# Two gate tiles computed from the input before its norm, and the decays' chain moved into the first pairs, in a one-core hybrid layer

## The chip, the cores and the metric

The kernel runs on one core of a Trainium2 chip. The metric is the device time of one execution in microseconds (us). TensorE (PE in the profile's rows; PEld is its weight load) multiplies matrices into PSUM, VectorE (DVE) and ScalarE (ACT) do elementwise work, GpSimd (POOL) does almost nothing here, and SyncE (SP) issues the loads and stores.

## The reference, cut to what matters

One layer over 2048 positions of 1024 features, in float32:

```python
h = rmsnorm(x, norm_mix_w)                     # x * rsqrt(mean(x*x) + eps) * norm_mix_w
proj = h @ w_in
u_b, u_c, u_h, z, xbc, dt_raw = split(proj)
y_a = u_b * causal_conv3(u_c * u_h)
xs, bm, cm = split(silu(causal_conv4(xbc) + bias))
dt = softplus(dt_raw + dt_bias)                # 16 heads; decays come from cumsum(dt * a) in chunks
y = ssd_scan(xs, dt, a, bm, cm) + d * xs
y_b = grouped_rmsnorm(y * silu(z)) * ssd_norm_w
x = x + concat(y_a, y_b) @ w_out
out = rmsnorm(x + square(relu(rmsnorm(x) @ w_up)) @ w_down)
```

The norm's root is one number per position. A column of `x * norm_mix_w` times a matrix, multiplied by that number afterwards, is the same as the product of the normalised column.

## The kernel before

**Precision.** Each float32 operand is split into a rounded part (`hi`: `uh` for activations, `whi` for weights, a copy on ACT) and a remainder (`lo`: `ul`, `wlo`, a subtraction on DVE). `mm3` (L113 to L115) makes one product out of three matmuls: `whi*uh`, `whi*ul`, `wlo*uh`. `split_w` is at L100 (ACT) and L101 (DVE), the split of activations at L204 and L205.

**Halves, blocks, pairs.** The sequence is two halves of 1024 positions, each two blocks of 512 (`bb` 0 and 1). Features lie on partitions, 8 slices of 128 (`k`), and a weight tile is 1024 x 128. The input projection works on *pairs* of weight tiles by a scheme of seven products instead of eight over two blocks and two tiles (`chain`, L269 to L271: seven products of four slices, 84 matmuls of 512 columns). The pairs are named by kind: `z` (gate, SiLU), `x` (the scan's convolution: six passes on DVE, L651), `ch` (short convolution's input), `b` (its multiplier). `first_half` runs them in the order of `PAIRS`; while one pair runs, the weights of the next are split, and after each of the seven products a hook lets a generator take one step: `late` is the preparation of the second half's blocks (squares L347, sums L349 and L352, root and reciprocal L170 and L171, scaling L368, differences L208). In the last pair the hook also refills the activation tiles for the second half (L319, L320).

**The start.** `start` loads block 0 and the weights of the first four `z` tiles (24 to 27), which are not done as pairs but as plain products (`group`), because the first pair's sums over both blocks do not exist yet. `begin_block` is a generator: squares (L448 for block 0, L453 for block 1), sums of squares (`acc`, L455 and L458), sum over partitions on PE (`reduce`, tile `pst`, L131), root, reciprocal and two diagonal tiles (`root`, L143 to L151), spread over all partitions by two matmuls (`spread`, tile `prb`, L177, copied to `facc` at L180), then for each slice the scaling by root and `norm_mix_w` in place (L467) and the split. `group(0)` multiplies three tiles, then the fourth; `dt_part` follows for block 0: 16 small-output matmuls into `pd` (L591) with the split weight `wdt` (L571, L572), a copy `dts<-pd` (L595), transposes (`pt`), some 25 small instructions on DVE for softplus, cumulative sums by a matmul (`pc`), exponentials, and stores. Meanwhile block 1 goes through `begin_block`; then `begin_sums` builds the sums over the blocks while `group(1)` runs, and `dt_part` for block 1 goes on into the first pair.

**Order.** The lines of code are issued in the order in which the generators are stepped; a scheduler then fixes an order for each engine's queue when the kernel is built, and each engine works its queue off in that order. Tiles come from rings of buffers, and a tile's new owner waits for the last reader of the old one: three raw weight tiles (`wraw`), four split ones, four `utmp` tiles for squares, diagonals and z, two `tp` banks of PSUM for the small products.

Of the kernel before, what the change touches and what calls it, by code (L numbers as in the profile page):

```python
# [11 lines left out]
F32 = mybir.dt.float32  # L12
# [11 lines left out]
KD = D // P  # L24
# [15 lines left out]
def trunk(ctx: ExitStack, tc: tile.TileContext, x, w_in, w_dt, w_out, w_up, w_down, cvec, hrow, out):  # L40
# [352 lines left out]
    class Proj(Seven):  # L393
# [1 line left out]

        stored = hm_d

        PAIRS = "ch0 ch1 b0 x0 x8 ch2 ch3 b2 x2 ch4 ch5 b4 x4 x10 ch6 ch7 b6 x6 z4 z6".split()
        LATER = "z0 x0 z4 ch0 ch1 b0 x8 ch2 ch3 b2 x2 ch4 ch5 b4 x4 x10 ch6 ch7 b6 x6 z6 z2".split()
        FIRST = {"z": 24, "x": 32, "b": 0}  # L400

# [35 lines left out]
            return self.e(name).rearrange("p (a t) -> p a t", a=2)  # L437


        def begin_block(self, bb):  # L440

            xt = self.xt[bb]
            st = Rstd(self.up, self.tmp, D, TB)
            acc = self.facc()
            for m, t in enumerate(xt):
                if bb == 0:
                    sq = self.wide("sq")
                    nc.scalar.activation(sq, t, AF.Square)  # L448
                    sq = [sq[:, 0], sq[:, 1]]
                else:  # L450
                    sq = [acc if m + i == 0 else self.tmp("sq") for i in range(2)]
                    for i in range(2):
                        nc.scalar.activation(sq[i], t[:, i], AF.Square)  # L453
                if m == 0:
                    nc.vector.tensor_tensor(out=acc, in0=sq[0], in1=sq[1], op=ALU.add)  # L455
                else:
                    for i in range(2):
                        nc.vector.tensor_tensor(out=acc, in0=acc, in1=sq[i], op=ALU.add)  # L458
                yield
            st.reduce(acc)  # L460
            st.root()
            yield
            r = st.spread(acc)
            yield
            for k in range(KD):
                t = xt[k // 2][:, k % 2]
                nc.vector.scalar_tensor_tensor(  # L467
                    out=t, in0=t, scalar=col(C_NMIX, k), in1=r, op0=ALU.mult, op1=ALU.mult
                )
                self.fill(("b11", "b21", "b12", "b22")[2 * bb + k // 4], k % 4, t)  # L470
                yield
# [25 lines left out]
                if k % 2:  # L497
                    yield

        def group(self, bb, ws, tiles, work, tag="mm"):  # L500

            pm = [psum(tag, "pm", accs[tag]) for _ in tiles]
            for k in range(KD):
                for p, i in zip(pm, tiles):
                    mm3(p, ws[i][0][:, k, :], ws[i][1][:, k, :], *self.block(bb, k), k, KD)
                next(work, None)
            for p, i in zip(pm, tiles):
                o = self.tmp("z")
                nc.scalar.activation(o, p, AF.Silu)
                nc.sync.dma_start(sz_d[0][:, i, bb * TB : (bb + 1) * TB], o)  # L510

        def start(self):

            self.xt = [[self.raw("x0") for _ in range(KD // 2)], []]
            for k, t in zip(range(0, KD, 2), self.xt[0]):
                nc.sync.dma_start(t, x[0, :, k : k + 2])
            ahead = self.plain(w_in, (24, 25, 26))
            next(ahead)
            work = self.begin_block(0)
            for m in range(KD // 2):  # L520
                next(work)
            for m in range(KD // 2):
                t = self.wide("x1")
                nc.sync.dma_start(t, x[1, :, 2 * m : 2 * m + 2])
                self.xt[1].append(t)
            next(work)
            ws = []
            for _ in range(3):
                ws += take(ahead, 1)
                next(work)  # L530
            self.dt_weights()
            for _ in work:
                pass
            work = self.begin_block(1)
            last = self.plain(w_in, (27,))
            next(last)
            for bb in range(NBB):
                dts = self.dt_part(bb)
                self.group(bb, ws, (0, 1, 2), work)
                if bb == 0:  # L540
                    ws += take(last)
                    self.group(bb, ws, (3,), work, "mw")
                    self.bias()
                    for _ in dts:
                        next(work, None)
                    for _ in work:
                        pass
                    work = self.begin_sums()
                else:
                    ahead = self.weights(0, self.PAIRS[0])  # L550
                    next(ahead)
                    next(dts)
                    got = take(ahead, 3)
                    self.group(bb, ws, (3,), work, "mw")
                    got += take(ahead)
                    for _ in dts:
                        next(work, None)
                    for _ in work:
                        pass
            return got  # L560

        def dt_weights(self):
# [214 lines left out]
        def first_half(self, ws):  # L777
            self.last_sums()
            late = self.prepare(1, x, C_NMIX)
            for m, what in enumerate(self.PAIRS):  # L780
# [8 lines left out]

                def after(name):  # L790
                    next(late, None)
                    if last:
                        self.refresh(name)

# [811 lines left out]
```

## Time and profile before

| | us |
|---|---|
| median of 3 runs | 2670.18 (2669.47 to 2673.78) |
| the profiled execution | 2667.12 |
| its span in the trace | 2665.4 |
| PE busy | 2603.0 (98%) |
| DVE busy | 1911.8 (72%) |
| ACT busy | 1432.6 (54%) |
| PE's first matmul of a tile | at 19.68 |
| PE's first matmul of a pair | at 76.64 |

All times of the trace count from the span's start. A row of a timeline gives start, duration, engine, line, operation and operands, and in brackets how long the engine had been idle and what ended that. Matmuls overlap in the trace: what one costs in a run of them is the distance of their starts, not the duration shown.

### The profile page before, as it was taken

To read this page: it belongs to the slowest core of one execution; us is meant where nothing else is said; L and a number is where in the kernel's file an instruction comes from. 1 tells how busy PE (TensorE), PEld (TensorE's weight loads), DVE (VectorE), ACT (ScalarE), POOL (GpSimd) and SP (SyncE) were. 2 spreads that over 40 slices of the span, in tenths; PEclk is the share of its full clock that TensorE was granted. 3 is DMA by queue.
4 is the path that set the end of the run, shared out by engine and by line. 5 is a ranking of instruction groups with operands and counts; after the bars stand their busy time and mean duration, and the time that the engine had idled before them with its cause. 6 is when DMAs were issued, how large, how long until landed. Compare 5 with 4: busy or idle time off the path is not lost. (4 is left out here: it accounts for less than half of the span.)

```text
span 2665.4 us, 33577 instructions
## 1 busy us (share of the span) xinstructions
PE 2603.0 (98%) x12026; PEld 2125.4 (80%) x12026; DVE 1911.8 (72%) x2586; ACT 1432.6 (54%) x2176; POOL 145.0 (5%) x162
## 2 busy tenths in 40 slices
PE   7999999999999999998998999999999999999998
PEld 5778888778887888787887888788887888888887
DVE  7997677667667666666659755765558877888985
ACT  6644345766567566757316555755555444444443
POOL 0000000011111001111000000000000000000001
PEclk9999999999999999999999999999999999999999
DMA  3585335655555589876597944644448554665762
GB/s 145 188 307 188 136 142 187 191 164 170 173 161 171 165 265 266 251 213 210 187 323 260 331 154 162 223 173 160 143 165 283 159 158 146 208 215 169 246 206 70
DMA packets 288262, 522.27 MB, mean 196 GB/s; under 512 B 25696, under 2 KB 141408, under 8 KB 288096
## 3 DMA queue, kind: packets, MB, share of 16 engines
q1 hardware_dynamic: 288096, 520.14, 58.6%
q8 instruction: 94, 1.54, 0.2%
q14 instruction: 72, 0.59, 0.1%
HBM read 349.65 MB, written 170.39 MB: 195 GB/s over the span
## 5 line engine op out<-in xcount | busy, mean ns | idle before, releaser
L269 PE MATMUL px<-uh,whi 128*128 128x512 f32 x1672 | 657.4, 393 | 10.4 <-ACT pw L277 5.4
L271 PE MATMUL px<-uh,wlo 128*128 128x512 f32 x1672 | 651.8, 390 | 2.1 <-DVE wlo L101 2.1
L270 PE MATMUL px<-ul,whi 128*128 128x512 f32 x1672 | 651.9, 390 | 0.0
L101 DVE TENSOR_TENSOR wlo<-wraw,whi 128x1024 fp32r<-128x1024 f32 x230 | 234.5, 1020 | 209.2 <-ACT whi L100 203.6
L269 PEld LDWEIGHTS px<-uh,whi 128*128 128x128 f32 x1672 | 314.4, 188 | 86.0 <-ACT pw L277 8.0
L100 ACT CAST whi<-wraw 128x1024 fp32r<-128x1024 f32 x230 | 204.0, 887 | 316.3 <-PE px L270 189.2
L271 PEld LDWEIGHTS px<-uh,wlo 128*128 128x128 f32 x1672 | 314.3, 188 | 69.2 <-DVE wlo L101 2.9
L270 PEld LDWEIGHTS px<-ul,whi 128*128 128x128 f32 x1672 | 314.4, 188 | 63.8
L269 PE MATMUL py<-uh,whi 128*128 128x512 f32 x836 | 326.9, 391 | 1.9 <-DVE acc L973 1.6
L270 PE MATMUL py<-ul,whi 128*128 128x512 f32 x836 | 325.6, 389 | 0.0
L100 ACT CAST whi<-s 128x1024 fp32r<-128x1024 f32 x210 | 219.7, 1047 | 197.0 <-PE py L270 69.6
L271 PE MATMUL py<-uh,wlo 128*128 128x512 f32 x836 | 325.4, 389 | 0.0
L101 DVE TENSOR_TENSOR wlo<-s,whi 128x1024 fp32r<-128x1024 f32 x210 | 255.6, 1217 | 84.8 <-ACT whi L100 81.5
L113 PE MATMUL pm<-uh,whi 128*128 128x512 f32 (+1 forms) x648 | 253.1, 392 | 2.1 <-ACT uh L204 2.1
L114 PE MATMUL pm<-ul,whi 128*128 128x512 f32 (+1 forms) x648 | 250.3, 386 | 0.0
L115 PE MATMUL pm<-uh,wlo 128*128 128x512 f32 (+1 forms) x648 | 249.9, 386 | 0.0
L269 PEld LDWEIGHTS py<-uh,whi 128*128 128x128 f32 x836 | 156.9, 188 | 35.8 <-DVE acc L973 2.0
L271 PEld LDWEIGHTS py<-uh,wlo 128*128 128x128 f32 x836 | 156.9, 188 | 33.0 <-DVE wlo L101 0.3
L270 PEld LDWEIGHTS py<-ul,whi 128*128 128x128 f32 x836 | 157.0, 188 | 32.2
L269 PE MATMUL pw<-uh,whi 128*128 128x512 f32 x418 | 163.5, 391 | 0.7 <-ACT pw L277 0.7
L270 PE MATMUL pw<-ul,whi 128*128 128x512 f32 x418 | 162.7, 389 | 0.0
L271 PE MATMUL pw<-uh,wlo 128*128 128x512 f32 x418 | 162.7, 389 | 0.0
(221 smaller groups left out, 3744.7 us busy)
## 6 DMA issues: line engine op xcount, KB each, us to landing
hid_d<-e SPq DMA_DIRECT2D x96, 512.0 KB, 4.7
rh<-hid_d SPq DMA_DIRECT2D x96, 512.0 KB, 4.4
wraw<-w_in SPq DMA_DIRECT2D x68, 512.0 KB, 4.0
wraw<-w_up SPq DMA_DIRECT2D x64, 512.0 KB, 4.4
wraw<-w_down SPq DMA_DIRECT2D x104, 256.0 KB, 3.7
dec<-rd_d SPq DMA_DIRECT2D x32, 512.0 KB, 5.4
wraw<-w_out SPq DMA_DIRECT2D x32, 512.0 KB, 5.0
x_d<-xt SPq DMA_DIRECT2D x64, 256.0 KB, 3.3
```

Of the source, the lines that this page charges most:

```text
L100: nc.scalar.copy(hi, raw)
L101: eng.tensor_tensor(out=lo, in0=raw, in1=hi.bitcast(F32), op=ALU.subtract)
L113: nc.tensor.matmul(out, whi, hi, start=(k == 0), stop=False)
L114: nc.tensor.matmul(out, whi, lo, start=False, stop=False)
L115: nc.tensor.matmul(out, wlo, hi, start=False, stop=(k == nk - 1))
L269: nc.tensor.matmul(p, hi, h[0], start=bool(first and k == 0), stop=False, **kw)
L270: nc.tensor.matmul(p, hi, h[1], start=False, stop=False, **kw)
L271: nc.tensor.matmul(p, lo, h[0], start=False, stop=(k == len(g) - 1), **kw)
```

## The change

`unscaled` makes the split of `x * norm_mix_w` for the eight slices of block 0, without the norm's root: `hi` by a multiply on ACT, `lo` in one DVE instruction that multiplies and subtracts. It puts them where block 1's slices will lie later. The first two `z` tiles are multiplied from these (`group` with `block`), and each of the two results is multiplied by the spread root (`self.r`) on DVE as it leaves PSUM, ahead of the SiLU. Tile 24's weights are loaded directly after the first quarter of block 0; tiles 26 and 27 are multiplied from the normalised block. The weights of the decays (`dt_weights`) are made after that; of `dt_part` only the first step (the 16 matmuls and the copy `dts<-pd`) is issued in `start`, and the rest goes step by step into the hooks of the first pairs. In `PAIRS`, `z4` and `x0` come first and `x6` is now the last but one.

```diff
-        PAIRS = "ch0 ch1 b0 x0 x8 ch2 ch3 b2 x2 ch4 ch5 b4 x4 x10 ch6 ch7 b6 x6 z4 z6".split()
+        PAIRS = "z4 x0 ch0 ch1 b0 x8 ch2 ch3 b2 x2 ch4 ch5 b4 x4 x10 ch6 ch7 b6 x6 z6".split()
...
+        def unscaled(self, k, t):
+
+            i, j = WHERE["b12" if k < 4 else "b22"]
+            p = self.places[k % 4]
+            p[i] = self.place(i)
+            hi, lo = (a[:, j] for a in p[i])
+            nc.scalar.mul(hi, t, col(C_NMIX, k))
+            nc.vector.scalar_tensor_tensor(
+                out=lo, in0=t, scalar=col(C_NMIX, k), in1=hi.bitcast(F32), op0=ALU.mult, op1=ALU.subtract
+            )
+            return hi, lo
...
         def begin_block(self, bb):
...
+            if bb == 0:
+                self.first = [self.unscaled(k, xt[k // 2][:, k % 2]) for k in range(KD)]
+                yield
             st.reduce(acc)
             st.root()
             yield
-            r = st.spread(acc)
+            r = self.r = st.spread(acc)
             yield
...
-        def group(self, bb, ws, tiles, work, tag="mm"):
+        def group(self, bb, ws, tiles, work, tag="mm", block=None):
...
-                    mm3(p, ws[i][0][:, k, :], ws[i][1][:, k, :], *self.block(bb, k), k, KD)
+                    hi, lo = block[k] if block else self.block(bb, k)
+                    mm3(p, ws[i][0][:, k, :], ws[i][1][:, k, :], hi, lo, k, KD)
                 next(work, None)
             for p, i in zip(pm, tiles):
                 o = self.tmp("z")
+                if block:
+                    nc.vector.tensor_tensor(out=o, in0=p, in1=self.r, op=ALU.mult)
+                    p = o
                 nc.scalar.activation(o, p, AF.Silu)
...
         def start(self):
...
-            for k, t in zip(range(0, KD, 2), self.xt[0]):
-                nc.sync.dma_start(t, x[0, :, k : k + 2])
-            ahead = self.plain(w_in, (24, 25, 26))
-            next(ahead)
+            load = lambda m: nc.sync.dma_start(self.xt[0][m], x[0, :, 2 * m : 2 * m + 2])
+            load(0)
+            ahead = [self.plain(w_in, (24,)), self.plain(w_in, (25, 26))]
+            next(ahead[0])
+            for m in range(1, KD // 2):
+                load(m)
+            next(ahead[1])
+            ahead = itertools.chain(*ahead)
             work = self.begin_block(0)
...
+            ws = take(ahead, 1)
             next(work)
-            ws = []
-            for _ in range(3):
-                ws += take(ahead, 1)
-                next(work)
-            self.dt_weights()
+            ws += take(ahead, 1)
+            next(work)
+            next(work)
+            last = self.plain(w_in, (27,))
+            next(last)
+            self.group(0, ws, (0, 1), work, block=self.first)
+            ws += take(ahead)
+            ws += take(last)
             for _ in work:
                 pass
+            self.dt_weights()
+            self.bias()
+            dts = [self.dt_part(bb) for bb in range(NBB)]
+            next(dts[0])
             work = self.begin_block(1)
-            last = self.plain(w_in, (27,))
-            next(last)
-            for bb in range(NBB):
-                dts = self.dt_part(bb)
-                self.group(bb, ws, (0, 1, 2), work)
-                if bb == 0:
-                    ws += take(last)
-                    self.group(bb, ws, (3,), work, "mw")
-                    self.bias()
-                    for _ in dts:
-                        next(work, None)
-                    for _ in work:
-                        pass
-                    work = self.begin_sums()
-                else:
-                    ahead = self.weights(0, self.PAIRS[0])
-                    next(ahead)
-                    next(dts)
-                    got = take(ahead, 3)
-                    self.group(bb, ws, (3,), work, "mw")
-                    got += take(ahead)
-                    for _ in dts:
-                        next(work, None)
-                    for _ in work:
-                        pass
+            self.group(0, ws, (2,), work)
+            self.group(0, ws, (3,), work, "mw")
+            for _ in work:
+                pass
+            work = self.begin_sums()
+            self.group(1, ws, (0, 1, 2), work)
+            ahead = self.weights(0, self.PAIRS[0])
+            next(ahead)
+            next(dts[1])
+            got = take(ahead, 3)
+            self.group(1, ws, (3,), work, "mw")
+            got += take(ahead)
+            for _ in work:
+                pass
+            self.dts = itertools.chain(*dts)
             return got
...
                 def after(name):
                     next(late, None)
+                    next(self.dts, None)
```

## The prediction

> **What bounds the kernel now.** I read the page first, then the timelines of ScalarE (ACT), VectorE (DVE) and TensorE (PE) over the first 110 us, where the change lies, then the waits and the busy time by stretch of the pairs that follow.
>
> ```profile
> span 2665.4 us, 33577 instructions
> PE 2603.0 (98%) x12026; PEld 2125.4 (80%) x12026; DVE 1911.8 (72%) x2586; ACT 1432.6 (54%) x2176; POOL 145.0 (5%) x162
> ```
>
> PE is the bound: what is to be won are the spots where it stands still or runs slowly. The largest in the edited code is the start. In the timelines' rows (start, duration, engine, line, operation, count, idle time before and what ended it) ACT comes first, then DVE, then PE.
>
> ```profile
> 5.88 1.06 ACT L448 ACTIVATE sq<-x 128x1024 f32<-128x1024 f32 x1 [3.59 <-DMA x<-x]
> 10.91 1.05 ACT L100 CAST whi<-wraw 128x1024 fp32r<-128x1024 f32 x1 [0.21 <-DMA wraw<-w_in]
> 11.98 1.28 ACT L143 ACT_TABLE_LOAD   x1
> 17.61 0.59 ACT L180 COPY facc<-prb 128x512 f32<-128x512 f32 x1 [0.82 <-PE prb L177]
> 19.01 0.62 ACT L204 CAST uh<-x 128x512 fp32r<-128x512 f32 x1 [0.29 <-DVE x L467]
> ```
>
> ```profile
> 6.97 0.69 DVE L455 TENSOR_TENSOR facc<-sq 128x512 f32<-128x512 f32 x1 [5.83 <-ACT sq L448]
> 8.21 4.46 DVE L458 TENSOR_TENSOR facc<-facc,sq 128x512 f32<-128x512 f32 x6 [0.55 <-ACT sq L448]
> 15.43 1.29 DVE L151 TENSOR_TENSOR diag<-ident,rs 128x512 fp32r<-128x512 f32 x2
> 18.89 1.22 DVE L101 TENSOR_TENSOR wlo<-wraw,whi 128x1024 fp32r<-128x1024 f32 x1
> 24.76 2.73 DVE L467 SCALAR_TENSOR_TENSOR x<-x,cv,facc 128x512 f32<-128x512 f32 x4
> 27.41 2.49 DVE L205 TENSOR_TENSOR ul<-x,uh 128x512 fp32r<-128x512 f32 x4
> ```
>
> ```profile
> 12.73 1.87 PE L131 MATMUL pst<-ones_r,facc 128*128 128x1 f32 x8 [12.73 <-DVE facc L458]
> 16.17 1.40 PE L177 MATMUL prb<-diag,ones_r 128*128 128x512 f32 x2 [1.57 <-DVE diag L151]
> 19.68 1.65 PE L113 MATMUL pm<-uh,whi 128*128 128x512 f32 x3 [2.12 <-ACT uh L204]
> 24.97 0.63 PE L114 MATMUL pm<-ul,whi 128*128 128x512 f32 x1
> 25.39 0.55 PE L115 MATMUL pm<-uh,wlo 128*128 128x512 f32 x1
> 26.25 0.40 PE L114 MATMUL pm<-ul,whi 128*128 128x512 f32 x1
> 26.48 0.40 PE L115 MATMUL pm<-uh,wlo 128*128 128x512 f32 x1
> ```
>
> PE gets its first product at 19.68 us, after squares, sum, root, spread and scaling. Until about 25.7 two starts lie 0.42 us apart (24.97 to 25.39), later 0.23 (26.25 to 26.48): half the rate. Then it runs almost without a hole to the first pair, while the next norm (block 1) hides behind group 0:
>
> ```profile
> 39.01 0.92 PE L131 MATMUL pst<-ones_r,facc 128*128 128x1 f32 x7
> ...
> 76.64 0.50 PE L269 MATMUL px<-uh,whi 128*128 128x512 f32 x1
> ```
>
> ```profile
> 43.98 0.59 ACT L180 COPY facc<-prb 128x512 f32<-128x512 f32 x1 [1.84 <-PE prb L177]
> 45.44 0.63 ACT L204 CAST uh<-x 128x512 fp32r<-128x512 f32 x1
> 49.78 0.58 ACT L595 COPY dts<-pd 32x512 f32<-32x512 f32 x1 [2.13 <-issue]
> ```
>
> **The change, step by step.** I walk the queues in the order of the built changed kernel, with the durations above. In a run of equal instructions the next starts 0.67 us after the last for scaling on DVE (2.73 for four), 0.60 for a difference, sum or diag, 1.14 for a wlo (1.22 less the overlap); on ACT 0.53 (512 wide) and 0.95 (1024).
>
> *Start.* The five loads of 512 KB came between 5.88 and 10.91, 1.26 us apart; weight 24 now comes second, at 7.1. ACT: square to 6.9, two uh to 8.0, whi to 9.0. DVE must now do eight ul beside the eight sums: per slice k a ul and a sum, 1.27 us. The first ul ends at 8.3, the second at 9.0, wlo at 10.2, then ul2 to ul7 at 11.5, 12.75, 14.0, 15.25, 16.5, 17.8; the sum of squares is whole at 17.1 (before: 12.7). PE starts at 9.0, 10.7 us earlier, but three products per k at the half rate take 1.28 us, no faster than DVE delivers; at 18.0, 22 products and pst have gone through, which at full rate are 22 x 0.23 + 0.8 = 5.8 us of work. So 3.2 of the 9.0 us are lost.
>
> *Norm of block 0.* Root at 18.3 (its table load stands behind the two whi at 17.0), wlo of 25 and 26 between, diag to 21.7, copy to 22.9: 4.7 us later than the copy that ended at 18.2. PE covers this with the rest of tiles 0 and 1, 26 products plus prb, done at 24.6. That cover is not quite long enough: ul of the scaled block comes at 26.3, and DVE then owes 8 scalings (5.3), 8 ul (4.8), two multiplies out of PSUM (1.2, by the 0.6 of a sum), wlo of 27 (1.14) and about 1.1 of small ones: 13.5 us, to 36.4. PE waits for ul (1.2 at 25, 1.5 near 30, 1.6 near 34) and wlo (0.6): 5.0 us together. Group 0 and the 16 pd of the decays are through at 44.2; the two multiplies are in that 13.5. On SP the load of w_dt now stands behind those of tile 27 and of the first pair's weights and waits for a diag buffer; by the 1.26 us a load it lands near 24 and is wanted at 35, so it costs nothing unless it is 11 us late. POOL has no part in it.
>
> *Norm of block 1: the new wait.* On ACT the copy dts<-pd stands ahead of seven of the eight squares of block 1. pd needs wdt, at the end of that DVE queue, so it runs from 36.7 to 40.3, the squares from 40.9 to 44.7 and the sums to 45.9. PE has by then run out of work: behind the last product of tile 3 stand pst, prb and only then block 1. From 45.9: pst 0.8, root and small ones 0.8, diag 1.3, prb 0.5, copy 0.6 (after a 1.28 us table load and a z, which fit beside it), scaling 0.75, uh 0.62: first product at 51.4. So 44.2 to 51.4 is empty but for 1.2 us: 6.0 us lost. Before, this chain took 39.01 to 46.1 and hid behind tile 3 and pd.
>
> *The clock after it.*
>
> ```profile
> 1216.97:1220.38 3.41, 1.26 (x7) 1.13 (x8) 3.30 (x5) 3.39 (x5) 0.49 (x1) 1.00 0.75 216
> 1220.40:1223.80 3.40, 3.40 (x9) 2.64 (x8) 2.99 (x3) 2.50 (x5) 2.29 (x2) 0.50 0.96 246
> ```
>
> In these rows (stretch, then busy us of PE, PEld, DVE, ACT, POOL, granted clock) PE was busy 1.26 of 3.41 us, and in the next 3.4 us it had half the clock. The new wait holds 1.2 us of work in 7.2 us, so half the clock for 3.4 to 6 us after it, about 2.0 us lost; 0 if it stays up, 3 if it takes longest. The Trainium skill ("TensorE: Matmul & The Clock Gate", Part 1, The two states you'll see) gives half rate only after at least one idle window of about 3.4 us, and by that rule, with pst and prb inside, the 2.0 would be 0. The trace disagrees: a stretch that was 37% busy was enough. The same section's free-running window agrees with the steps of 3.4 us here.
>
> *Sum to the first pair.* Before: 76.64. Less 19.7 at the start, about 2.7 at half rate (13 products at 0.20) and 0.7 in small gaps, that is 53.5 us of PE work (with the second pst and prb). The changed kernel does the same, 1.0 less for pc, pr and one pt that go among the pairs, 1.2 more for the first pst and prb, which now lie inside: 53.7. Then 9.0 + 53.7 + 3.2 + 5.0 + 6.0 + 2.0 = 78.9, and the 1.0 comes later: **3.3 us behind**. Bounds: 1.3 (no half clock) to 5.3 (the clock comes up only behind the first pst, which puts the first norm 2 us later).
>
> *The first pairs.* A pair is 84 products x 0.227 = 19.1 us. DVE is the near-bound there:
>
> ```profile
> L101 DVE TENSOR_TENSOR wlo<-s,whi 128x1024 fp32r<-128x1024 f32 x14 | 17.1, 1223 | 0.6 <-ACT whi L100 0.4
> L651 DVE SCALAR_TENSOR_TENSOR cacc<-buf,cv,cacc 128x1024 f32<-128x1024 f32 x12 | 15.4, 1282 | 0.0
> L368 DVE SCALAR_TENSOR_TENSOR nb<-nb,cv,facc 128x512 f32<-128x512 f32 x16 | 11.3, 746 | 0.2 <-DMA nb<-x 0.2
> L208 DVE TENSOR_TENSOR nb<-nb 128x512 f32<-128x512 f32 x16 | 10.5, 686 | 0.0
> L171 DVE RECIPROCAL facc<-facc 128x512 f32<-128x512 f32 x2 | 6.7, 3347 | 0.0
> ```
>
> ```profile
> 96.29 0.22 DVE L619 SCALAR_TENSOR_TENSOR dts<-dts 128x64 f32<-128x64 f32 x1
> 96.42 0.69 DVE L696 TENSOR_TENSOR cc<-py,s 128x512 f32<-128x512 f32 x1
> ```
>
> ```profile
> 134.00:154.00 20.00, 20.00 (x90) 16.57 (x89) 13.84 (x21) 4.77 (x7) 0.57 (x1) 1.00 0.74 277
> 154.00:173.00 19.00, 17.95 (x78) 14.18 (x77) 19.00 (x25) 11.03 (x14) 2.34 (x3) 1.00 0.77 273
> 173.00:193.00 20.00, 17.89 (x78) 14.17 (x77) 19.80 (x27) 10.42 (x13) 2.24 (x3) 1.00 0.93 354
> ```
>
> ```profile
> PE px L271 <- DVE wlo L101: 2.1, 2, 1.5
> ```
>
> The views are the groups by line, a piece of DVE's timeline, the busy time by stretch and the waits. From 154 to 193 DVE is full and PE lacks 1.05 + 2.11 us, mostly waiting for wlo; a stall also hides some 0.16 us of the last product's modelled end, so about 4.5 us in all can come back. Why there: x0 and x8 (six L651 each, 7.7 us) meet there with the second half's preparation (L368, L208). In the new order z4, which has neither, comes first and x8 sixth, and the decays' two chains (some 25 small instructions at 0.13, 96.29 to 96.42, about 3.5 us each) move in. Every pair costs DVE 7.6 us (three wlo and a half one 4.0, four half sums 2.4, two adds 1.2); x0 in second place adds 7.7, a chain 3.5, a reciprocal 3.3, seven sums and a lo of the preparation 4.8: 27 us against 19.1. But DVE enters the pairs 3.5 us nearer to PE than before, and walking its queue I find every wlo of pairs 2 to 4 in time, by little; the one for b0's second product stands behind eight nb steps of the pair before and comes at about 161 where 159 is wanted. The chains' own pc has 0.4 us to spare on PE; what DVE is later than that, PE waits. Their ten small stores now lie among the loads of lx on SP; nothing reads them in this half. So I take 2 us of stalls for the 4.5: **2.5 us back**; bounds 4.5 back and 2 worse.
>
> *End of the first half.* x6 now stands last but one, so up to 7.7 us of L651 fall into the pair in which DVE refills the next block:
>
> ```profile
> 460.00:480.00 20.00, 18.07 (x78) 14.11 (x77) 15.96 (x19) 15.39 (x22) 0.00 (x0) 1.00 0.84 284
> ```
>
> ```profile
> PE px L269 <- ACT s L693: 1.4, 1, 1.4
> ```
>
> DVE has 4.0 of 20 us free, so it may end 3.7 late. PE waits only through ACT's queue (the 1.4 us): **1.2 us lost**, bounds 0 and 3.7.
>
> **Sum:** 3.3 - 2.5 + 1.2 = 2.0 us slower. The profiled execution took 2667.12 (span 2665.4 and 1.7 around it); it lies 3.06 under the median of 2670.18, which becomes about **2672.2**. A difference under 0.2% (5.3 us) cannot be told from none by a measurement of this kernel, whose three runs spread over 4.3 us.
>
> **Rivals.**
> 1. *The start's gain stays* (faster). If block 1's squares reach ACT before pd, or pst fits ahead of tile 3's end, the 6.0 and the 2.0 are gone: 2664.2. For it: the scheduler's order was meant to hide this. Against: pst stands behind tile 3's last product, and the squares behind dts<-pd. Chance 0.07.
> 2. *DVE becomes the bound in pair 2* (slower). With x0 and both chains, DVE's 27 us exceed the pair by 7.9; it takes 3.5 from its lead, and the rest, 4.4, is PE's as soon as wlo for pair 3 is later than its first product. Nothing comes back, so 2.0 + 2.5 + 4.4 = 8.9: 2679. For it: the full DVE rows above. Against: x's sums can trail behind wlo. Chance 0.15.
> 3. *Both ends of the half and the slow clock cost more* (first norm 2 us later, refill 3.7 late): 2.0 + 2.0 + 2.5 = 6.5: 2676.7. Chance 0.10.
> 4. *No half clock after the new wait*: 2.0 back: 2670.2. For it: the wait is not quite empty, 1.2 us of work lie in it; against it the 1216.97 row. The Trainium skill's rule named above speaks for it. Chance 0.13.
> 5. *Weight 24 lands no earlier than its 10.91* although issued second, and the early products do little: start 2 us later, 2674. Against: loads land in order here. Chance 0.05.
>
> **How the numbers follow.** My forecast has the remaining 0.50, at 2672.2, with its own range 2669 to 2675. The range over all, 2667.5 to 2678.5, takes in rivals 3 to 5, and the bound of 4.5 back; it leaves out rival 1 and the upper part of rival 2. Faster by over 0.2% is rival 1: 0.07. Slower by over 0.2% is rivals 2 and 3, less what falls short, 0.23 in all. The rest, 0.70, is within 0.2%.
>
> **What would show it.** First product near 9 us; facc<-prb near 23; the second pst near 46 with PE empty for some 6 us around it and half the clock behind; the first px near 79; PE's lack in the first seven pairs about half of before's. I am wrong if the second pst comes before tile 3 ends, or if DVE's wlo holds PE in pairs 2 and 3 for more than 2 us.

## The result, and the profile after

| | before | after |
|---|---|---|
| median, 9 runs each | 2670.22 us (2664.28 to 2676.84) | 2682.49 us (2676.19 to 2692.42) |
| the profiled execution | 2667.12 | 2682.08 |

The ratio is 1.0043, 95% interval 1.0031 to 1.0055: slower by some 12 us, where the forecast was 2 and the range ended at 2678.5. The direction was right, the size was not.

The page of the changed kernel, its span and its line of busy time:

```profile
span 2680.1 us, 33586 instructions
PE 2608.6 (97%) x12026; PEld 2126.4 (79%) x12026; DVE 1918.0 (72%) x2596; ACT 1439.0 (54%) x2186; POOL 146.4 (5%) x162
```

PE does the same 12026 matmuls; its busy time grew by 5.6 us, the span by 14.7. So 5.6 us of the difference show as longer busy time and 9.1 as standing still, and the question is where.

**The start.** TensorE's timeline of the changed kernel: the first product, the last product of block 0, then the second sum, its spread, block 1's first products, and the first pair:

```profile
9.23 0.79 PE L113 MATMUL pm<-uh,whi 128*128 128x512 f32 x1 [9.23 <-ACT whi L100]
...
44.48 0.39 PE L115 MATMUL pm<-uh,wlo 128*128 128x512 f32 x1
47.68 1.45 PE L131 MATMUL pst<-ones_r,facc 128*128 128x1 f32 x8 [2.81 <-DVE facc L470]
50.78 1.31 PE L177 MATMUL prb<-diag,ones_r 128*128 128x512 f32 x2 [1.66 <-DVE diag L151]
54.20 1.65 PE L113 MATMUL pm<-uh,whi 128*128 128x512 f32 x3 [2.11 <-ACT uh L204]
...
82.26 0.39 PE L269 MATMUL px<-uh,whi 128*128 128x512 f32 x1
```

The walk through block 0 came out as forecast (first product 9.23 for 9.0; the copy of the first spread, in the next fence, ends at 23.22 for 22.9; the last product, starting at 44.48, is through near 44.7 for 44.2). From there on PE has nothing but the sum and its spread until 54.20, 2.8 us later than the forecast 51.4. ScalarE's and VectorE's timelines say why:

```profile
22.63 0.59 ACT L180 COPY facc<-prb 128x512 f32<-128x512 f32 x1 [2.94 <-PE prb L177]
...
41.01 0.58 ACT L616 COPY dts<-pd 32x512 f32<-32x512 f32 x1 [5.04 <-PE pd L612]
41.49 2.82 ACT L465 ACTIVATE sq<-x 128x512 f32<-128x512 f32 x5
44.48 0.63 ACT L465 ACTIVATE sq<-x 128x512 f32<-128x512 f32 x1 [0.17 <-DVE facc L470]
```

```profile
42.15 0.69 DVE L467 TENSOR_TENSOR facc<-facc,sq 128x512 f32<-128x512 f32 x1 [4.74 <-ACT sq L465]
42.95 4.67 DVE L470 TENSOR_TENSOR facc<-facc,sq 128x512 f32<-128x512 f32 x6
49.95 1.29 DVE L151 TENSOR_TENSOR diag<-ident,rs 128x512 fp32r<-128x512 f32 x2
```

ACT stood idle for 5.04 us before `dts<-pd`, with seven squares queued behind it; DVE, idle for 4.74 us, waited for those squares. The place of the wait is the forecast one. The sums then end at 42.95 + 4.67 = 47.62, where 45.9 had been forecast. The squares don't hold them up: five are done by 44.31, when the third sum is still running, and the last two wait for a buffer that a sum must free (the 0.17 <-DVE facc). The sums set the pace, 0.80 us from start to start ((4.67 - 0.69) / 5) instead of the forecast 0.60. The kernel before has the same step:

```profile
34.04 3.08 DVE L458 TENSOR_TENSOR facc<-facc,sq 128x512 f32<-128x512 f32 x4
```

Each of these sums reads the `facc` that the one before it wrote. In block 0 of the changed kernel, where a residual `ul` follows each sum, the `ul` starts 0.60 us after the sum (10.35 to 10.95). That the dependence makes the difference is read from these rows and was not tried by itself.

The busy time by stretches of 3.4 us, laid on the steps of the granted clock (stretch, then busy us of PE, PEld, DVE, ACT, POOL, the clock, DMA):

```profile
44.80:48.20 3.40, 0.58 (x6) 0.52 (x5) 2.51 (x4) 2.22 (x3) 0.00 (x0) 1.00 0.01 2
48.20:51.60 3.40, 1.74 (x7) 1.41 (x6) 1.71 (x5) 2.14 (x3) 0.00 (x0) 0.50 0.00 0
51.60:55.00 3.40, 1.29 (x3) 0.70 (x3) 2.25 (x4) 2.46 (x5) 0.00 (x0) 0.50 0.40 154
55.00:58.40 3.40, 3.40 (x11) 2.14 (x11) 3.40 (x6) 1.51 (x3) 0.00 (x0) 0.50 0.00 0
```

Half the clock lasts from 48.2 to 58.4. So it catches the second sum (1.45 us against 0.92 for seven of its eight before) and the spread too, not only block 1's products.

**The first seven pairs.** Below, pair starts are counted in the trace, 84 matmuls of L269 to L271 a pair. The stretch from the first product to the eighth pair, of before and then of the changed kernel:

```profile
76.60:217.80 141.20, 137.52 (x599) 110.99 (x599) 129.71 (x184) 72.27 (x94) 10.98 (x14) 1.00 0.73 264
```

```profile
82.30:224.10 141.80, 138.44 (x607) 111.39 (x606) 131.09 (x202) 79.62 (x104) 8.32 (x13) 1.00 0.76 270
```

The stretch is 0.6 us longer (0.7 from the exact starts): PE stands still for 3.36 us instead of 3.68, and has 0.92 more of work, the chains' small products. The forecast was 2.5 less standing still. The waits of that stretch show that its cause did change:

```profile
PE px L269 <- ACT s L714: 1.2, 1, 1.2
PE px L269 <- ACT pw L277: 0.7, 1, 0.7
PE pw L269 <- ACT pw L277: 0.7, 1, 0.7
PE pc L649 <- DVE dts L643: 0.6, 1, 0.6
```

None for `wlo`, which held PE before; instead ScalarE and the chain's own `pc`.

**The end of the first half.** From the second half's first pair, the 21st, over four pairs: 105.7 us before (466.2 to 571.9), 111.6 after (472.6 to 584.2). In it TensorE waits for long on two things, the copy `pw` and, at two places, the decays' `dts`:

```profile
PE px L269 <- ACT pw L277: 3.6, 1, 3.6
PE pc L649 <- DVE dts L643: 3.1, 2, 1.6
```

Before, the longest there are 2.1 us for `dts` and 1.4 on ACT. The clock drops behind the wait for `pw`, from 481.7 to 485.1, and behind the second wait for `dts`, from 549.9 to 553.3 (before it doesn't drop in this stretch). The first drop:

```profile
478.00:481.60 3.60, 0.25 (x2) 0.00 (x0) 1.96 (x3) 1.53 (x3) 0.00 (x0) 1.00 1.00 395
481.60:485.00 3.40, 3.13 (x7) 2.48 (x8) 2.79 (x4) 1.45 (x3) 0.00 (x0) 0.51 0.88 287
```

The copy `pw` stands on ACT behind the cast of a reloaded tile, and that waits for its load. ACT's timeline, then the reloads on SP's queue (start, and the time its instructions took), of the changed kernel:

```profile
480.29 1.04 ACT L319 CAST uh<-rb 128x1024 fp32r<-128x1024 f32 x1 [2.07 <-DMA rb<-hm_d]
481.24 0.58 ACT L277 COPY pw<-px 128x512 f32<-128x512 f32 x1
```

```profile
460.09 2.65 SPq L312 DMA_DIRECT2D rb<-hm_d  x2
...
463.56 11.37 SPq L312 DMA_DIRECT2D rb<-hm_d  x6
```

and SP's queue before:

```profile
452.25 8.17 SPq L312 DMA_DIRECT2D rb<-hm_d  x6
```

Before, six reloads go out from 452.25. In the changed kernel, whose whole run there lies 6.4 us later, the first goes out at 460.09, 1.4 us late, the third at 463.56, 2.1 late, and the eighth at 474.61, 4.4 late (463.81 before). What holds them is VectorE. A reload overwrites a buffer that a subtraction `ul` (L320) read last, and each of the changed kernel's twelve reloads goes out 0.03 us after such a subtraction ends. VectorE's timeline of the changed kernel, then of before:

```profile
454.06 4.87 DVE L672 SCALAR_TENSOR_TENSOR cacc<-buf,cv,cacc 128x1024 f32<-128x1024 f32 x4
458.85 1.22 DVE L320 TENSOR_TENSOR ul<-rb,uh 128x1024 fp32r<-128x1024 f32 x1
459.98 1.28 DVE L672 SCALAR_TENSOR_TENSOR cacc<-buf,cv,cacc 128x1024 f32<-128x1024 f32 x1
461.18 3.49 DVE L320 TENSOR_TENSOR ul<-rb,uh 128x1024 fp32r<-128x1024 f32 x3
```

```profile
451.00 4.63 DVE L320 TENSOR_TENSOR ul<-rb,uh 128x1024 fp32r<-128x1024 f32 x4 [3.12 <-ACT uh L319]
```

In the changed kernel four passes of `x6`'s convolution (L672) stand ahead of the first subtraction and a fifth stands between it and the second. The queue's waits of the changed kernel say the same:

```profile
SPq L312 <- DVE ul L320: 13.9, 11, 3.0
```

Two stores of `x6`'s convolution also stand among the reloads on that queue, and the first waits 4.7 us for ScalarE. But they go out at 459.21 and 462.83, each before the next reload's buffer is free (460.07 and 463.53), so they hold nothing up. The expectations below still name these stores as the cause.

**Added up** by the milestones of the two profiled executions: first pair +5.6, eighth pair +6.3, 21st +6.5, 25th +12.3, last matmul +14.7. The last 2.4 have no place of their own: the code from the 25th pair on is the same in all versions, and in the profiled executions below this distance lies between 5.1 us under (e5) and 7.6 over (e8) that of before.

### The profile page after: what moved, and what is told of

It is laid out like the page before. It is cut to its first block, busy times and chain, and to the rows that moved or that the text cites. A ratio compares the mean times of both kernels' runs of the same rounds, so it can differ in the third digit from the quotient of the medians.

```text
span 2680.1 us, 33586 instructions
## 1 busy us (share of the span) xinstructions
PE 2608.6 (97%) x12026; PEld 2126.4 (79%) x12026; DVE 1918.0 (72%) x2596; ACT 1439.0 (54%) x2186; POOL 146.4 (5%) x162
## 4 chain that ended last, share of the span: by engine, by line
PE 56%; issue 26%; DMA 6%; DVE 6%; ACT 4%; POOL 1%; SPq 0%; POOLq 0%; DVEq 0%; ACTq 0%
PE px L269 9%; PE px L271 9%; PE px L270 9%; PE py L269 4%; PE py L270 4%; PE py L271 4%; PE pm L113 2%; PE pm L114 2%; PE pw L269 2%; PE pm L115 2%; PE pw L271 2%; PE pw L270 2%; DMA dec<-rd_d 1%; PE yd L1269 1%; DMA xt<-x_d 1%
## 5 line engine op out<-in xcount | busy, mean ns | idle before, releaser
L269 PE MATMUL px<-uh,whi 128*128 128x512 f32 x1672 | 658.9, 394 | 19.5 <-ACT pw L277 10.3
L271 PE MATMUL px<-uh,wlo 128*128 128x512 f32 x1672 | 652.4, 390 | 0.1
L269 PEld LDWEIGHTS px<-uh,whi 128*128 128x128 f32 x1672 | 315.0, 188 | 94.6 <-ACT pw L277 12.7
L271 PEld LDWEIGHTS px<-uh,wlo 128*128 128x128 f32 x1672 | 314.7, 188 | 67.4 <-DVE wlo L101 0.9
L269 PE MATMUL py<-uh,whi 128*128 128x512 f32 x836 | 327.0, 391 | 1.5 <-DVE acc L995 1.4
L271 PE MATMUL py<-uh,wlo 128*128 128x512 f32 x836 | 325.5, 390 | 0.0
L269 PEld LDWEIGHTS py<-uh,whi 128*128 128x128 f32 x836 | 156.9, 188 | 35.4 <-DVE acc L995 1.8
L271 PEld LDWEIGHTS py<-uh,wlo 128*128 128x128 f32 x836 | 156.9, 188 | 33.4 <-DVE wlo L101 0.6
L269 PE MATMUL pw<-uh,whi 128*128 128x512 f32 x418 | 163.5, 391 | 0.7 <-ACT pw L277 0.7
L271 PE MATMUL pw<-uh,wlo 128*128 128x512 f32 x418 | 162.8, 390 | 0.0
```

The costliest lines, as they stand in the source:

```text
L269: nc.tensor.matmul(p, hi, h[0], start=bool(first and k == 0), stop=False, **kw)
L271: nc.tensor.matmul(p, lo, h[0], start=False, stop=(k == len(g) - 1), **kw)
```

## The experiments

My theory at this point: two things cost, the decays' products and copy ahead of block 1's squares, and `x6` next to the refill. The rival: the early start, the order or the decays among the pairs cost by themselves, whatever stands where. What each expects of a run, as its A and B, is quoted with it. All runs are in one table; "8th" and "25th" are pair starts in the profiled execution, less those of before (217.84 and 571.90). The ratio is to the kernel before, run on the same chip; the runs were not all on one chip, so between two versions the ratios compare better than the medians.

| run | median us | ratio (95%) | 8th | 25th |
|---|---|---|---|---|
| after | 2682.49 | 1.0043 (1.0031 to 1.0055) | +6.3 | +12.3 |
| e1_squares_first | 2676.03 | 1.0026 (1.0016 to 1.0036) | -0.4 | +5.7 |
| e2_x6_earlier | 2678.34 | 1.0033 (1.0020 to 1.0046) | +5.5 | +5.6 |
| e3_both | 2673.75 | 1.0010 (1.0001 to 1.0019) | +0.2 | +2.1 |
| e4_order_alone | 2673.94 | 1.0011 (1.0001 to 1.0021) | -2.1 | +0.9 |
| e5_border_x6 | 2666.98 | 0.9986 (0.9974 to 0.9997) | -3.7 | -2.4 |
| e6_three_early | 2672.92 | 1.0005 (0.9994 to 1.0016) | +1.3 | +2.8 |
| e7_decays_in_start | 2671.67 | 1.0007 (0.9997 to 1.0016) | -0.4 | +0.3 |
| e8_warm | 2687.75 | 1.0066 (1.0049 to 1.0083) | +8.7 | +12.5 |
| e9_start_alone | 2673.18 | 1.0016 (1.0005 to 1.0026) | +2.6 | +3.4 |
| e10_decays_alone | 2668.77 | 0.9999 (0.9990 to 1.0008) | -2.9 | -2.3 |
| e11_residuals_on_gpsimd | 2679.69 | 1.0033 (1.0019 to 1.0046) | +7.1 | +6.7 |

**Decays behind block 1's squares** (from the changed kernel):

```diff
             dts = [self.dt_part(bb) for bb in range(NBB)]
-            next(dts[0])
             work = self.begin_block(1)
             self.group(0, ws, (2,), work)
             self.group(0, ws, (3,), work, "mw")
+            next(dts[0])
```

> The changed kernel with one statement moved: the first step of block 0's decays (the 16 pd matmuls and the copy dts<-pd) is issued after group 0 instead of before it, so that block 1's squares stand ahead of the copy on ACT and 14 of the 16 pd stand behind prb on PE. Theory A (block 1's norm was exposed by that copy): the second pst starts near 42 us instead of 47.7, pd fills the wait between prb and the first product of block 1, the clock stays up, the first px comes near 76 instead of 82.3, and the time falls by 5 to 7 us. Theory B (DVE's added work of eight ul and two multiplies, 6.5 us, is what costs): the first px moves by less than 2 us and the time by less than 2.

TensorE's timeline of this run has the second sum 5.1 us earlier:

```profile
42.58 1.02 PE L131 MATMUL pst<-ones_r,facc 128*128 128x1 f32 x8 [1.54 <-DVE facc L470]
45.18 0.54 PE L177 MATMUL prb<-diag,ones_r 128*128 128x512 f32 x1 [1.57 <-DVE diag L151]
```

Block 1's first product comes at 51.0, half the clock lasts 3.4 us instead of 10.2, the eighth pair starts 6.7 us earlier and the median is 6.5 lower (by the two ratios 0.17%, some 4.5 us). That is Theory A for the squares, but for the clock, which it expected to stay up. It does not make the early start a gain: the first pair starts where it did before (76.53 to 76.64), and the sum is still 3.6 us later than before's 39.01.

**`x6` three places further from the refill:**

```diff
-        PAIRS = "... x4 x10 ch6 ch7 b6 x6 z6".split()
+        PAIRS = "... x4 x10 x6 ch6 ch7 b6 z6".split()
```

> The changed kernel with x6 moved from the last place but one to four places earlier in PAIRS, so that b6 stands before z6. Theory A (the stores of x6's convolution, which wait for ACT, hold the refill's loads back on SP's queue): the 3.6 us wait for pw near 478 us and the half clock behind it go, the first 84 products of the second half are back to some 28.6 us, and the time falls by 3 to 6 us. Theory B (the second half's start is late for DVE's load alone): the wait stays at over 2 us.

The four pairs after the half take 105.7 us, exactly as before; there is no wait for `pw` of that size, and the clock does not drop. SP's queue in this run:

```profile
457.85 8.21 SPq L312 DMA_DIRECT2D rb<-hm_d  x6
```

Six reloads go out in one run again. The median is 4.2 us lower (by the ratios 0.10%, some 2.7). So `x6`'s place is the cause: a wait for `pw` of over 3 us stands in all four profiles with `x6` last but one (the changed kernel, e1, e4, e8) and in none of the others. Theory A's reason, the stores, does not hold: the edit takes `x6`'s passes on VectorE away from there together with the stores, and by the rows above the passes held the reloads. Theory B names the right engine, but its load moved too.

**Both edits together:**

> Both edits together. Theory A: the two costs lie in different places, so the gains add, 8 to 13 us under the changed kernel, that is, within 4 us of the kernel before or below it. Theory B: they do not add, and the time stays over 2676.

At the milestones the gains add (the eighth pair as with the first edit; the four pairs take 107.3 us, 1.6 more than with the second, with one drop of the clock at 540.3), and 8.7 us of the median go: Theory A. What is left over is small, +0.10%, but not a gain.

**The order alone** (the kernel before with the changed `PAIRS`):

> The kernel before with only the new order of the pairs (z4 and x0 first, x6 last but one); start and decays as before. Theory A: the end of the half costs 3 to 6 us as in the changed kernel, and the first pairs give back at most 1: 2672 to 2676. Theory B (the order was worth its change in the first pairs): 2667 to 2671.

Theory A by the time and the half's end, but the order by itself gives 2.1 us back in the first seven pairs, where A allowed at most 1. It then pays at the half's end, with the same wait as in the changed kernel:

```profile
PE px L269 <- ACT pw L277: 3.1, 1, 3.1
```

So the 2.5 us that I had forecast for the order are nearly there, but not in the changed kernel. **The order with `x6` moved, old start:**

```diff
-        PAIRS = "ch0 ch1 b0 x0 x8 ch2 ch3 b2 x2 ch4 ch5 b4 x4 x10 ch6 ch7 b6 x6 z4 z6".split()
+        PAIRS = "z4 x0 ch0 ch1 b0 x8 ch2 ch3 b2 x2 ch4 ch5 b4 x4 x10 x6 ch6 ch7 b6 z6".split()
```

> The kernel before with the new order of the first half and x6's convolution one place earlier (z4 x0 ... x10 x6 ch6 ch7 b6 z6); start and decays' chains as before. Theory A (the order by itself gives some 2.1 us back in the first seven pairs, and what the order alone lost was the wait for rb at the half's end): first px at 76.7, pair 7 at 215.7, first pair to the first of the second half, then four more pairs in 105.7 instead of 109.4, so some 2 us under before: 2667 to 2668.5. Theory B (the order's gift of the first pairs is taken back further on whatever stands at the half's end): 2669.5 to 2672, no different from before.

Theory A, and the only version that beats both kernels: 2666.98 us, 0.14% under before (0.03 to 0.26%). Its profiled execution, 2659.63, was the fastest of its twelve. Its first seven pairs:

```profile
75.60:214.10 138.50, 136.73 (x600) 111.13 (x600) 126.31 (x179) 78.54 (x100) 10.96 (x13) 1.00 0.76 275
```

PE stands still for 1.77 us there, against 3.68 before. One us of its 3.7 at the eighth pair is from a start that happened to be earlier (75.65), and is not the order's: the clock came up at 23.8 us there and at 25.7 before, so 1.9 us less ran at half the rate, in the same code.

**Three tiles instead of two without the norm** (from e3_both):

```diff
-            self.group(0, ws, (0, 1), work, block=self.first)
...
+            self.group(0, ws, (0, 1, 2), work, block=self.first)
...
-            self.group(0, ws, (2,), work)
```

> The changed kernel with the squares' sums before the decays, x6 earlier, and three tiles of z (24, 25, 26) instead of two from the block without its norm; only tile 27 takes the normalised block. Theory A (the waits for the cast and the residual of the normalised block in tiles 2 and 3 are short of other work on TensorE, and a third tile's 24 products per block pair cover them): first px 1.5 to 3 us earlier than 76.7, time 2670 to 2672 against 2673.8 of the version with two. Theory B (the start is bound by VectorE's walk through block 0, which the third tile does not shorten and its multiply lengthens): first px 76.5 to 77.5, time as with two tiles.

Theory B: the start is no earlier (first pair 77.06), and the time is as with two tiles (2672.92 against 2673.75). The three short waits for `ul` became one for the last weight's remainder (waits), while DVE never stopped (the stretch of that wait):

```profile
PE pm L115 <- DVE wlo L101: 5.9, 1, 5.9
```

```profile
32.40:35.80 3.40, 0.00 (x0) 0.00 (x0) 3.40 (x7) 2.41 (x3) 0.00 (x0) 1.00 0.00 0
```

The second sum came at 44.7 instead of 42.7. Giving PE more to do early doesn't help when the queue that feeds it is full: VectorE is the bound of this start.

**The decays' chains run out in the start** (from e3_both, `next(dts[0])` and `next(dts[1])` become loops to their end, none in the hooks):

> The changed kernel with the squares' sums before the decays and x6 earlier, and both chains of the decays run out in the start, as before, none among the pairs. Theory A (the chain in the pairs eats what the new order gives): first px 77.5 to 78.5 (1 to 1.5 us of small products more in the start), first pair to pair 7 in 139.0 instead of 141.4, time 2671.5 to 2673, 1 us under the version with the chain in the pairs. Theory B (the chain costs the pairs nothing): first pair to pair 7 stays at 141 to 141.5, time 2674.5 to 2675.5.

The first pair starts at 73.42, 3.3 earlier than in e3_both, because its products overtake block 1's decays in PE's order; its start is no measure here, and my forecast of 77.5 to 78.5 and of 139.0 for the pairs missed both ways. The eighth pair, with all small work done in both, starts 0.7 us earlier, and the median is 2.1 lower (by the ratios 0.03%, 0.8 us), within Theory A's 2671.5 to 2673. That the chains' place is worth some 1 us is likely, not certain: the two intervals overlap.

**Idle products under the slow clock** (from the changed kernel):

```diff
+            warm = psum("tp", "warm", 2)
+            for _ in range(26):
+                nc.tensor.matmul(warm, ws[3][0][:, 0, :], self.block(0, 0)[0], start=True, stop=True)
```

> The changed kernel with 26 products more, into a bank that nothing reads, issued behind block 1's spread sum, where TensorE stands thin. They leave the result as it is and add 26 x 0.23 = 6 us of TensorE work at full clock, most of it in idle time. Theory A (some 4 to 5 us of the half clock's stretch, 48.2 to 58.4, go away because TensorE is busy there): half clock gone or begun later, first px at 80 to 82. Theory B (the dip is set by the thin stretch before the second sum, 44.5 to 48, which the products don't fill): half clock from 48.2 as in the changed kernel, first px 83 to 86, time 2683 to 2686.

Theory B by the first pair (84.60) and by the drop, which the products don't prevent; the time lies over both theories. The products land behind the spread, at 50.60 to 59, and block 1 waits behind them. Half the clock starts at 48.7 (48.2 in the changed kernel) and ends at 55.5 (58.4):

```profile
48.70:52.10 3.40, 2.06 (x5) 1.70 (x6) 1.72 (x5) 1.88 (x2) 0.00 (x0) 0.50 0.19 76
52.10:55.50 3.40, 3.40 (x9) 2.63 (x9) 2.76 (x5) 2.95 (x5) 0.00 (x0) 0.50 0.20 78
55.50:58.90 3.40, 3.40 (x16) 2.77 (x16) 3.40 (x6) 1.50 (x3) 0.00 (x0) 0.99 0.00 0
```

Behind the full stretch 52.10 to 55.50 the clock is back, one step earlier than in the changed kernel. The eighth pair is 2.4 us later than in the changed kernel. The run doesn't settle how many us the clock alone cost there.

**The early start alone** (e7_decays_in_start with the old `PAIRS`):

> The early start alone: tiles 24 and 25 from the block without its norm, the squares' sums of block 1 ahead of the decays, both decays' chains run out in the start, and the order of the pairs as before. Theory A (the early start costs by itself, since VectorE's walk is longer by eight residuals and two multiplies; the run with the new order, x6 earlier and this start was 4.7 us over the run with the old start): pair 7 at 219 to 221 against 217.8 before, 2673 to 2675.5. Theory B (with the sums first the start is worth nothing either way, and the 4.7 us are the two runs' other differences): pair 7 at 217 to 218.5, 2669.5 to 2672.

Theory A, at its lower end: +0.16%, the eighth pair 2.6 us later than before. With the order of e5 on both sides, e7 against e5, the same step is 3.3 us, of which 1.0 is e5's chance start.

**The decays alone** (e5 with only the products and the copy in the start, the rest in the hooks):

> The old start with the order that was fastest so far (x6 earlier) and, of the decays, only the products and their copy in the start; the rest of both chains goes to the pairs, one step behind each name. Theory A (the chain in the pairs takes back most of what the order gives there): first seven pairs 1 to 2 us longer than 138.5, 2668.5 to 2670.5. Theory B (it costs the pairs nothing, and the start is rid of 18 small products): 2666 to 2667.5.

```profile
73.70:214.90 141.20, 139.04 (x612) 111.69 (x611) 128.65 (x198) 77.81 (x102) 8.42 (x13) 1.00 0.75 268
```

The stretch is 2.7 us longer than in e5 (1 to 2 were expected), and its start 1.9 earlier: 0.8 us net at the eighth pair. PE stands still for 2.16 us in it, 0.4 more than in e5. Theory A by the median, +1.8, but the intervals overlap, and at the 25th pair nothing is left of it. The chains' price is small, and its size is not settled.

**The residuals on GpSimd** (from e7_decays_in_start):

```diff
-            nc.scalar.mul(hi, t, col(C_NMIX, k))
-            nc.vector.scalar_tensor_tensor(
-                out=lo, in0=t, scalar=col(C_NMIX, k), in1=hi.bitcast(F32), op0=ALU.mult, op1=ALU.subtract
-            )
+            nc.scalar.mul(t, t, col(C_NMIX, k))
+            nc.scalar.copy(hi, t)
+            nc.gpsimd.tensor_tensor(out=lo, in0=t, in1=hi.bitcast(F32), op=ALU.subtract)
```

> The early start with the sums first, decays in the start and x6 earlier (2671.7 us), but the eight residuals of the block without its norm go from VectorE to GpSimd: ScalarE scales the input in place, copies it to the high part, and GpSimd subtracts; the norm's multiply then leaves the weight out. Theory A (VectorE's walk sets when block 1's second sum and its normalised block come; 8 x 0.747 us = 6.0 us of it go): second sum 38 to 40 instead of 42.6, pair 7 at 212 to 215 against 217.4, 2666 to 2669. Theory B (ScalarE, with eight passes more, or GpSimd at some 1.4 us a residual takes VectorE's place): pair 7 at 217 to 220, 2671 to 2674.

Theory B, and worse than it: 8 us over e7. ACT is full from 14 to 24 us, and the first spread's copy comes at 28.23:

```profile
14.00:24.00 10.00, 7.80 (x21) 5.64 (x21) 6.66 (x8) 9.97 (x17) 9.39 (x6) 1.00 0.70 231
```

So this run tells that ScalarE has no room for eight passes, and, in the last section, that GpSimd's subtractions slowed VectorE, which was to be relieved. That the start would gain if VectorE were relieved without loading another engine was not shown.

## Why the prediction was wrong, point by point

The forecast's terms came to 2.0 us, all ahead of the 25th pair, and the profiles show 12.3 there. Of the 10.3 between them, 3.4 lie ahead of the first pair, 2.2 in the first seven pairs and 4.7 at the end of the half.

- **Start and norm of block 0: right.** First product 9.23 (9.0), end of the spread's copy 23.22 (22.9), block 0 through near 44.7 (44.2). The clock came up earlier than I had walked with: starts lie 0.43 us apart until 13.64 and 0.23 from 14.06, where I had half the rate until 18.0. It changed nothing, since VectorE sets the pace there: 22 products and the sum were through at 18.4.
- **Norm of block 1: right place, wrong size, by 2.8 us.** Sums end 47.62 (45.9): the copy came 0.7 later than my 40.3, and from there the sums took 1.0 more, since I costed them at 0.60 us a step and they take 0.80, as they do before (34.04 above). The second sum took 1.45 (0.8), and from the end of the diagonals, 51.24, the second spread took till its copy at 52.13, 0.9 (0.5), both at half the clock: I let the dip begin behind the wait, and it began inside it. First product 54.20 (51.4). The dip itself lasted 10.2 us where I had 3.4 to 6; of the products it halved 54.2 to 58.4, that is 2.1 us (2.0).
- **To the first pair:** 82.26 (78.9; bound 76.64 + 5.3 - 1.0 = 80.9). The 3.4 us are the 2.8 and some small gaps. e1 shows what the copy ahead of the squares costs: with the squares first, 6.7 us go at the eighth pair.
- **The first pairs: 2.5 us back, measured 0.3 of standing still.** The reason given, `wlo` off the path, was right, and the order alone does give 2.1 (e4) or 1.9 of standing still (e5). What failed is the sum: I let the order pay for the chains and took no price for ScalarE's queue, and in the changed kernel PE now waits there. In single profiles, the old order stands still for 3.68 us, the new one for 1.77 (e5), the new one with the chains for 2.16 (e10). With the new start as well it is 3.36 in the changed kernel and 2.77 in e2, but 1.91 in e1 and 2.16 in e3, where the squares come first. So by these the chains cost 0.4 and the early start by itself nothing; what took the rest back goes with the late norm of block 1.
- **End of the first half: 1.2 us, measured 5.9 over four pairs.** I let VectorE end up to 3.7 us late, but let TensorE feel only 1.2 of it, through ACT's queue. The step that I left out is the ring of buffers: a late subtraction frees its buffer late, so the reload goes out late, its cast comes late, and the copy `pw` stands behind that cast; TensorE waits 3.6 us. The clock, which I did not price there, drops behind this wait and once more behind a wait for `dts` (3.1 us in all, 2.1 before). e2 shows that moving `x6` takes all of it away in its profile. The second drop is not tied to `x6`'s place: e3 has it with `x6` moved, e4 does not have it with `x6` unmoved.
- **Rival 1** (squares ahead of the copy keep the start's gain, 2664.2) is the run e1: 2676. The condition was met and no gain came by the first pair (76.53 for 76.64); the rest of its time lies at the half's end (+5.7 at the 25th pair). In e1 VectorE works without a pause from 23.17 to 41.5, and the scaling that begins there began at 18.23 before; so I put the second sum's 3.6 us down to VectorE's eight residuals and two multiplies. No run that relieves VectorE alone shows it. **Rival 2** (VectorE the bound in pair 2) didn't come: no wait for `wlo`. **Rival 3** had the refill 3.7 us late, and that the wait came to 3.6 is in part luck, since the path to it was not walked; its first norm 2 us late did not come, and it left out the clock at the half's end. **Rival 4** (no half clock) is out, as is **rival 5** (weight 24 was cast at 8.15).
- **The clock's rule.** The Trainium skill ("TensorE: Matmul & The Clock Gate", Part 1, The two states you'll see) lets the rate fall only after an idle window of about 3.4 us. The traces disagree again: the stretch ahead of the drop held 0.58 us of 3.40, with 2.81 us as its longest idle time, and in e7 (last section) more than half. For the way up the same section asks for a busy window; with 55.00 to 58.40 fully busy and full rate right behind it, the trace agrees.

## What to carry to other kernels

Before starting early, see whether the engine that feeds the start has room: here TensorE's first product came 10.5 us earlier and block 1's norm, behind VectorE's longer walk, 3.6 us later even at best. When a step is moved, walk every in-order queue past it: a copy that waits for TensorE ahead of seven squares cost some 4 to 7 us. Walk the rings of buffers too: passes on VectorE ahead of the subtractions that free the reloads' buffers cost some 3 to 6 us at the end of the half, far from the start. Take bundled edits apart: the order with one pair moved, alone, was the only part that gained.

## What was not expected of the hardware

The clock falls after stretches that are far from idle. In e7, two neighbouring stretches:

```profile
33.10:36.50 3.40, 1.96 (x6) 1.12 (x7) 3.40 (x8) 3.31 (x5) 0.00 (x0) 1.00 0.00 0
36.50:39.90 3.40, 3.40 (x10) 2.63 (x9) 3.29 (x7) 2.42 (x4) 0.00 (x0) 0.50 0.90 236
```

1.96 us busy of 3.40 were followed by 3.4 us at half the clock. How a wait falls on the stretches matters as well: in e8 the wait for `pw` at the half's end, 3.1 us in one piece (480.65 to 483.74), lies half in one stretch and half in the next, and the clock stays up through both and behind them:

```profile
478.80:482.20 3.40, 1.84 (x9) 1.19 (x7) 3.32 (x3) 1.85 (x4) 0.00 (x0) 1.00 0.87 281
482.20:485.60 3.40, 1.86 (x8) 1.56 (x9) 2.37 (x4) 2.73 (x4) 0.00 (x0) 1.00 1.02 389
```

In e7's stretch ahead of the drop the longest idle time was 0.65 us. A busy share below which the clock drops can't be read from these runs.

And GpSimd slowed VectorE in e11; VectorE's timeline and groups while GpSimd subtracted, and GpSimd's own:

```profile
23.01 1.13 DVE L147 TENSOR_TENSOR rs<-rs,rs 128x4 fp32r<-128x4 f32 x1
```

```profile
L469 DVE TENSOR_TENSOR facc<-facc,sq 128x512 f32<-128x512 f32 x6 | 7.1, 1181 | 1.2 <-ACT sq L459 0.9
```

```profile
16.20 7.93 POOL L448 TENSOR_TENSOR ul<-x,uh 128x512 fp32r<-128x512 f32 x5 [0.16 <-ACT uh L447]
```

A sum that takes 0.68 us elsewhere took 1.18 on the mean, and four numbers a lane 1.13 us instead of 0.16; that one ended at 24.14, with GpSimd's last subtraction (24.13). The Trainium skill ("SBUF — State Buffer", SBUF: two separate sides) gives VectorE and GpSimd one shared pair of ports, held for a whole instruction, where VectorE reads two operands; these rows agree.
